# A hybrid decoder layer: low parts of the output weights moved behind the attention's divisions, first input blocks loaded in halves

## The chip, the cores and the metric

One NeuronCore of a Trainium2 chip runs the whole layer. The time is the device time of one execution in microseconds (us). TensorE multiplies matrices into PSUM; VectorE, ScalarE and GpSimd do elementwise work on SBUF (GpSimd not on PSUM); SyncE (SP) and ScalarE issue the transfers used here. Each engine takes its instructions in the order in which the program lists them.

## The reference

x is 512 x 1024, in float32. The layer is

```
h = rmsnorm(x, norm_g);  p = h @ w_in            # 1024 x 3380, split by columns
y_gla  = rmsnorm(gated linear attention(p)) * silu(gate)      # 4 heads, 384 channels
y_dsa  = sparse softmax attention(p) * silu(gate)             # 6 heads of 64
         # per query the 128 keys with the highest indexer score; softmax(q k / 8 + T5 bias)
y_pool = pooling mixer(p) * silu(gate)                        # 256 channels
out = rmsnorm(x + [y_gla, y_dsa, y_pool] @ w_out, final_norm_g)
```

## The kernel before, in words

Every product with a weight is made of three: an operand is split into a high part (a copy in the matmul's own format, `hi_of`, on ScalarE) and a low part (what the copy lost, `lo_of`, mostly on VectorE), and high x high, low x high and high x low are added in PSUM. 512 tokens are 4 tiles of 128, 1024 model columns are 8 blocks of 128.

**Opening** (`open_run`, L927). It multiplies the transposed, unnormalised x by the first 512 columns of w_in, block by block over the 8 blocks of the model dimension. Block k is a tile of x (128 x 512) and one of w_in (128 x 512). Block 0 of x comes with the 8 columns of norm_g behind it in one transfer (x0, L940); w0 and w1 are issued by ScalarE, all else by SP. Before its products TensorE runs four matmuls on ones (L991, 512, 512, 256 and 128 columns; each is two passes). `split(k)` (L949) makes the high part of w (whk, ScalarE), the high part of x times norm_g (hTh: VectorE for block 0, ScalarE for the others), the low part of x (hTl, VectorE) and the low part of w (wlk, VectorE). `square(k)` adds up x squared for the norm, on ScalarE and GpSimd. `products(k)` (L967) runs 3 x 4 matmuls of 512 columns.

**Projections** (`project`, L1017). The rest of w_in comes in chunks of some 256 columns, in the order qd, n1 to n4, dg, pg, c2, c1, pu, c0; each is loaded in two halves. Between the groups of matmuls a dictionary of hooks, `after` (L622), lists by hand what every engine is given next: ("pu", 0, "mid") is what comes in the middle of the first group of chunk pu, ("pu", 0) what comes after it. The order of these lists is the order of each engine's queue.

**Attention steps.** `att(...)` calls them by a letter, the query tile and the pair of heads ("n02" is n for tile 0, pair 2). l (L683): mask and bias into L, GpSimd, two instructions for tiles 2 and 3. q (L699): scores on TensorE, maximum on VectorE, exponentials with their sums on ScalarE. n (L715): reciprocal of the sums on VectorE (L719), then two multiplications on GpSimd (L721). t (L724): transposes of L on TensorE, copied out by ScalarE and VectorE. v (L734): values on TensorE (ov), times the gate on VectorE (yt), high part on ScalarE. y (L747): low part on VectorE.

**Output weights.** w_out comes in four chunks wo0 to wo3. `out_high(n, h)` (L901) makes the high parts of one half of chunk n on ScalarE, two instructions into tiles oh; `out_low(n, h)` (L909) the low parts ol, two instructions on VectorE. The tiles of the output weights take over memory that earlier tiles have left, so their first writes also wait for the last readers of those.

**Finish** (`finish`, L815). `out_part` adds the output products of one token tile: kinds G (linear attention), P (pooled, which wants yPh and yPl), D (softmax attention). Between them stand the attention steps of pairs 1 and 0 and the remaining parts of the weights, again in an order written out by hand. `pool_low` (L599) makes yPl, two VectorE instructions.

Of the kernel before, what the change touches and what calls it, by code (L numbers as in the profile page):

```python
# [69 lines left out]
def hybrid_layer(  # L70
# [16 lines left out]
    def S(tag, shape, dt=F32, bufs=1, name=None):  # L87
        return sb.tile(shape, dt, tag=tag, name=name or tag, bufs=bufs)
# [529 lines left out]
    def phase(n):  # L618
# [47 lines left out]
        ("c1", 1): [lambda: nc.gpsimd.memset(up[:, :, 0:16], 0.0), *att("l02", "l12"), partial(topk, 1, 3)],  # L666
        ("c1", 1, "end"): [*halves("c01"), partial(topk, 16, 2, 3)],
        ("pu", 0, "mid"): [*att("q02"), lambda: out_high(0, 0)],
        ("pu", 0): [lambda: out_low(0, 0), *att("n02", "q12")],
        ("pu", 1, "mid"): [*att("t02", "n12", "l22"), lambda: out_high(1, 0)],  # L670
        ("pu", 1): [*att("v02", "t12", "l32", "q22"), lambda: out_low(1, 0), lambda: pool_branch(0)],
        ("c0", 0, "mid"): att("n22", "y02", "v12", "q32"),
        ("c0", 0): att("t22", "n32", "l01"),
        ("c0", 0, "end"): [lambda: load_next(), *att("y12")],
        ("c0", 1, "mid"): [*att("v22", "t32", "l11"), lambda: pool_branch(1)],
# [139 lines left out]
    def finish():  # L815

        def do(*names):
            for f in att(*names):
                f()
# [12 lines left out]
        nc.sync.dma_start(lt["fg"], final_g.rearrange("(o d) -> o d", o=1).broadcast_to([P, D]))  # L832
        out_open(0), out_open(1)
        out_part(2, 0, T, "G", first=True)
        do("v01", "t11", "n21", "q00", "l10")
        pool_low()
        out_part(0, 0, T, "P")
        do("y01", "v11", "t21", "n00", "q31", "l20")
        out_low(2, 0)
        out_high(3, 0)  # L840
        out_part(1, 0, T, "P")
        do("y11", "v21", "t00", "n31", "q10", "l30")
        out_low(3, 0)
        out_high(2, 1)
        out_part(2, 0, T, "P")
        do("v00", "y21", "t31", "y00", "n10", "q20")
        out_low(2, 1)
        out_high(3, 1)
        out_part(0, 0, T, "D", last=True)
# [77 lines left out]
    def open_run():  # L927
# [3 lines left out]
        pns = [PS("ov", [P, T], 1, name="pf0"), PS("sc", [P, T], 2, name="pf1"), PS("sc", [P, T], 2, name="pf2"),  # L931
               PS("pj", [P, T], 3, name="pf3")]
        ht = lambda parts, k: parts[k // 4][:, k % 4, :]
        x0 = S("x0", [P, T + KT])
        g_of = lambda k: x0[:, T + k:T + k + 1]

        def load_x(k):
            if k == 0:
                xs[0] = x0[:, 0:T]
                nc.sync.dma_start(x0, block(x_t, 0, T + KT))  # L940
                return
            xs[k] = S("xk", [P, T], bufs=5, name=f"xk{k}")
            nc.sync.dma_start(xs[k], block(x_t, k * P * T + P * KT, T))

        def load_w(k, eng=nc.sync):
            ws[k] = S("wk", [P, T], bufs=5, name=f"wk{k}")
            eng.dma_start(ws[k], block(w_in, k * P * T, T))

        def split(k):  # L949
            wh[k] = S("whk", [P, T], F32R, bufs=3, name=f"whk{k}")  # L950
            wl[k] = S("wlk", [P, T], F32R, bufs=3, name=f"wlk{k}")
            hi_of(wh[k], ws[k])
            if k:
                nc.scalar.activation(ht(hTh, k), xs[k], AF.Copy, scale=g_of(k))
            else:
                nc.vector.tensor_scalar(ht(hTh, k), xs[k], g_of(k), None, op0=ALU.mult)
            nc.vector.scalar_tensor_tensor(ht(hTl, k), xs[k], g_of(k), ht(hTh, k).bitcast(F32),
                                           op0=ALU.mult, op1=ALU.subtract)
            lo_of(wl[k], ws[k], wh[k])
# [7 lines left out]
        def products(k, parts=range(3)):  # L967
            for part in parts:
                a, w = ht(hTl if part == 1 else hTh, k), (wl if part == 2 else wh)[k]
                for t in range(NT):  # L970
                    mm(pns[t], a[:, t * P:(t + 1) * P], w, start=(k + part == 0),  # L971
                                    stop=(k == KT - 1 and part == 2))

        def rms():

# [12 lines left out]
        nc.sync.dma_start(tab, table)  # L988
        load_next()
        load_next()  # L990
        for n in (4, 4, 2, 1):  # L991
            mm(warm[:, 0:n * P], ones, ones4[:, 0:n, :], start=True, stop=True)
        split(0)
        square(0)
# [76 lines left out]
def _x_blocks(x_t, norm_g):  # L1071

    import numpy as np

    first = np.concatenate([x_t[0:P], norm_g.reshape(KT, P).T], axis=1)
    return np.concatenate([first.reshape(-1), x_t[P:].reshape(-1)])


def _blocks(w, cols):
# [6 lines left out]
def _layout(i):  # L1086
    import numpy as np

    i = {n: np.asarray(a) for n, a in i.items()}
    w_in, w_out = i["w_in"][0], i["w_out"][0]  # L1090
    return {
        "in_x": i["x"],
        "in_x_t": _x_blocks(i["x"][0].T, i["norm_g"][0]),
        "in_w_in": np.concatenate([w_in[:, FIRST].reshape(-1)] + [_blocks(w_in, cols) for _, cols in CHUNKS]),
        "in_w_out": np.concatenate([_blocks(w_out, list(range(256 * j, 256 * j + 256))) for j in range(4)]),
        "in_rel_bias": _bias_layout(i["rel_bias"]),
        "in_table": _small_layout(i["gla_gate_w2"], i["gla_gate_b"], i["gla_norm_g"], i["pool_w"], i["pool_scale"]),
        "in_final_g": i["final_norm_g"],
    }
# [24 lines left out]
```

## Time and profile before

| | |
|---|---|
| median of 3 runs | 263.54 us (262.72 to 264.03) |
| the profiled execution | 262.61 us, span 260.7 us |
| mean granted clock of TensorE | 0.987 |
| TensorE busy | 245.6 us, 94% of the span |
| VectorE busy | 198.2 us, 76% |
| ScalarE, GpSimd busy | 119.0 us, 46%; 105.5 us, 40% |

In the rows, PE is TensorE, PEld its weight loads, DVE VectorE, ACT ScalarE, POOL GpSimd and SPq the issue of a transfer by SP. A row of a timeline gives start and duration in us, engine, line, operation, what is written from what, sizes, how many instructions are merged in it (x) and, in brackets, how long the engine was idle before it and whose result ended that. A matmul's row includes its way through the array, so rows of one engine overlap. PEclk is the share of TensorE's full clock that was granted.

### The profile page before, as it was taken

Reading aid. Unit: us, or ns where it says so; the run is one execution under the profiler, and the core shown is the slowest. Engines: PE = TensorE matmul, PEld = TensorE weight load, DVE = VectorE, ACT = ScalarE, POOL = GpSimd, SP = SyncE. Lnnn points to the kernel's source line nnn. Section 1 sums busy time; section 2 is a strip of 40 time slices with the busy share of each in tenths; the row PEclk is TensorE's granted clock in tenths of the full one; section 3 lists DMA queues with packets and bytes.
Section 4 is the critical chain, followed back from the end, with each engine's and each line's share of the span. In section 5 each row is a group of like instructions: output and inputs, shape, how many; then the busy total and the mean of one; then the engine's idle time right before and its main releaser. Section 6 shows DMA issues by size and latency. Waiting matters only on the chain.

```text
span 260.7 us, 4198 instructions
## 1 busy us (share of the span) xinstructions
PE 245.6 (94%) x1498; PEld 204.9 (79%) x1498; DVE 198.2 (76%) x442; ACT 119.0 (46%) x251; POOL 105.5 (40%) x109
## 2 busy tenths in 40 slices
PE   8999999999999999999999996699998989999990
PEld 4778889999999998778888884477875757778890
DVE  3999488999999999996999862288789797345322
ACT  5964186884836724062223452324168457222111
POOL 1644356253067730438534070534618783000011
PEclk9999999999999999999999999799999999999997
DMA  7994413226203150222325887500669000035012
GB/s 246 394 411 152 129 45 97 72 67 235 77 1 93 70 165 3 80 80 83 88 73 115 194 211 194 177 1 19 195 148 365 3 1 0 3 106 207 36 56 80
DMA packets 11780, 31.09 MB, mean 119 GB/s; under 512 B 1600, under 2 KB 1600, under 8 KB 11760
## 3 DMA queue, kind: packets, MB, share of 16 engines
q1 hardware_dynamic: 11328, 30.05, 36.2%
q10 hardware_dynamic: 432, 0.79, 0.8%
q8 instruction: 12, 0.20, 0.4%
q14 instruction: 8, 0.07, 0.1%
HBM read 23.91 MB, written 2.10 MB: 100 GB/s over the span
## 4 chain that ended last, share of the span: by engine, by line
PE 54%; DVE 30%; DMA 6%; issue 5%; POOL 2%; ACT 1%; POOLq 0%; ACTq 0%; DVEq 0%
PE op L772 14%; DVE scs L459 8%; DVE m L458 6%; PE pf L971 5%; PE pt_c L210 4%; PE pt_c L208 4%; PE pt_c L209 4%; DMA wr_wo<-in_w_out 3%; PE tpp L730 3%; PE ov L741 3%; PE ps L708 2%; DVE scs L444 2%; DMA wk<-in_w_in 2%; DVE wl_n L99 2%; PE pt_pg L210 1%
## 5 line engine op out<-in xcount | busy, mean ns | idle before, releaser
L721 POOL TENSOR_SCALAR L<-L,ast 128x128 f32<-128x128 f32 (+3 forms) x24 | 15.0, 639 | 32.5 <-DVE ast L719 32.5
L458 DVE MAX8 m<-scs 128x8 f32<-128x256 f32 (+2 forms) x48 | 26.5, 552 | 0.1
L459 DVE MATCH_REPLACE8 scs<-m,scs 128x256 f32<-128x256 f32 (+2 forms) x48 | 26.0, 543 | 0.0
L196 PE MATMUL pn_n<-wh_n,hTh 128*128 128x270 f32 (+1 forms) x128 | 21.6, 291 | 0.0
L196 PE MATMUL pn_n<-wl_n,hTh 128*128 128x270 f32 (+1 forms) x128 | 21.2, 287 | 0.0
L196 PE MATMUL pn_n<-wh_n,hTl 128*128 128x270 f32 (+1 forms) x128 | 21.0, 286 | 0.0
L208 PE MATMUL pt_c<-hTh,wh_c 128*128 128x512 f32 x48 | 19.2, 400 | 0.0
L210 PE MATMUL pt_c<-hTh,wl_c 128*128 128x512 f32 x48 | 19.0, 395 | 0.0
L209 PE MATMUL pt_c<-hTl,wh_c 128*128 128x512 f32 x48 | 18.9, 395 | 0.0
L196 PEld LDWEIGHTS pn_n<-wh_n,hTh 128*128 128x128 f32 x128 | 18.2, 189 | 0.7 <-issue 0.4
L712 ACT ACTIVATE L<-L,ast 128x128 f32<-128x128 f32 (+3 forms) x24 | 13.3, 554 | 11.8 <-DVE ast L710 10.7
L196 PEld LDWEIGHTS pn_n<-wl_n,hTh 128*128 128x128 f32 x128 | 18.0, 189 | 0.0
L196 PEld LDWEIGHTS pn_n<-wh_n,hTl 128*128 128x128 f32 x128 | 18.0, 189 | 0.0
L99 DVE TENSOR_TENSOR ol<-wr_wo,oh 128x512 fp32r<-128x512 f32 x16 | 12.8, 837 | 6.6 <-ACT oh L96 3.9
L99 POOL TENSOR_TENSOR wl_c<-wr_c,wh_c 128x1024 fp32r<-128x1024 f32 x5 | 12.0, 2401 | 12.9 <-PE pt_c L210 8.7
L730 PE MATMUL tpp<-ident,L 128*128 128x128 f32 x60 | 9.7, 288 | 6.3 <-POOL L L721 6.2
L965 POOL TENSOR_TENSOR acc<-acc,sqk 128x512 f32<-128x512 f32 x7 | 10.6, 1513 | 10.9 <-ACT sqk L963 10.8
L730 PEld LDWEIGHTS tpp<-ident,L 128*128 128x128 f32 x60 | 6.6, 142 | 9.4 <-POOL L L721 7.9
L96 ACT ACTIVATE yDh<-yt 128x128 fp32r<-128x128 f32 x12 | 3.7, 308 | 21.9 <-DVE yt L744 21.9
L558 POOL TENSOR_TENSOR gss<-gss,hneg 128x4 f32<-128x4 f32 x4 | 5.0, 1238 | 21.3 <-DVE gss L557 18.5
L778 ACT ACTIVATE sqo<-xr 128x512 f32<-128x512 f32 (+1 forms) x8 | 4.8, 605 | 17.9 <-DVE xr L777 12.9
L689 POOL TENSOR_TENSOR L<-scs,TB 128x512 f32<-128x512 f32 x9 | 12.9, 1438 | 0.0
(241 smaller groups left out, 710.7 us busy)
## 6 DMA issues: line engine op xcount, KB each, us to landing
wr_wo<-in_w_out SPq DMA_DIRECT2D x8, 512.0 KB, 4.2
wr_c<-in_w_in SPq DMA_DIRECT2D x6, 512.0 KB, 3.6
wr_n<-in_w_in SPq DMA_DIRECT2D x4, 540.0 KB, 7.8
wr_n<-in_w_in SPq DMA_DIRECT2D x4, 536.0 KB, 3.5
xr<-in_x SPq DMA_DIRECT2D x4, 512.0 KB, 6.0
xk<-in_x_t SPq DMA_DIRECT2D x7, 256.0 KB, 5.4
wk<-in_w_in SPq DMA_DIRECT2D x6, 256.0 KB, 5.2
KK<-qkh SPq DMA_DIRECT2D x12, 128.0 KB, 2.5
```

Source lines behind the costliest of these rows:

```text
L99: return (eng or nc.vector).tensor_tensor(dst, src, hi.bitcast(F32), op=ALU.subtract)
L196: mm(ps[:, 0:n], a[:, k, ts_], w[:, k, :], start=(h + part + k == 0), stop=(h == 1 and part == 2 and k == 3))
L208: mm(ps[:, t0:T], c.hi[h][:, k, cs], hTh[h][:, k, t0:T], start=(h + k == 0), stop=False)
L209: mm(ps[:, t0:T], c.hi[h][:, k, cs], hTl[h][:, k, t0:T], start=False, stop=False)
L210: mm(ps[:, t0:T], c.lo[h][:, k, cs], hTh[h][:, k, t0:T], start=False, stop=(h == 1 and k == 3))
L458: nc.vector.max(out=m8, in_=msk[i])
L459: nc.vector.match_replace(out=msk[i], in_to_replace=m8, in_values=msk[i], imm_value=TAKEN)
L712: nc.scalar.activation(L[:, b, 0:n], L[:, b, 0:n], AF.Exp, bias=st[:, b:b + 1], scale=-1.0, accum_out=st[:, 2 + b:3 + b])
L721: nc.gpsimd.tensor_scalar(L[:, b, 0:n], L[:, b, 0:n], st[:, 4 + b:5 + b], 1.0, op0=ALU.mult, op1=ALU.mult)
L730: nc.tensor.transpose(tp[:, kb, :], L[:, b, kb * P:(kb + 1) * P], ident)
L772: mm(outs[t][a][:, 0:e - a], lhs, rhs, start=(first and yi == 0 and rhs is wh and lhs is yh), stop=(last and yi == len(ys) - 1 and lhs is yl))
L971: mm(pns[t], a[:, t * P:(t + 1) * P], w, start=(k + part == 0), stop=(k == KT - 1 and part == 2))
```

## The change

In the hooks, out_low(0,0) moves from the start of ("pu", 0) to the end of ("pu", 1, "mid"), ahead of out_high(1,0); out_low(1,0) moves from ("pu", 1) to the end of ("c0", 0, "mid"). In the finish, pool_low moves ahead of v01, t11, n21, q00 and l10; l20 and l30 move to the end of the next lists. In the opening the first block of x (with norm_g now in front) and the first block of w_in come in two transfers of 256 columns each, their high parts are made in two halves and the first products in eight matmuls of 256 columns; the warm-up keeps its first two matmuls of four.

```diff
-        ("pu", 0): [lambda: out_low(0, 0), *att("n02", "q12")],
-        ("pu", 1, "mid"): [*att("t02", "n12", "l22"), lambda: out_high(1, 0)],
-        ("pu", 1): [*att("v02", "t12", "l32", "q22"), lambda: out_low(1, 0), lambda: pool_branch(0)],
-        ("c0", 0, "mid"): att("n22", "y02", "v12", "q32"),
+        ("pu", 0): att("n02", "q12"),
+        ("pu", 1, "mid"): [*att("t02", "n12", "l22"), lambda: out_low(0, 0), lambda: out_high(1, 0)],
+        ("pu", 1): [*att("v02", "t12", "l32", "q22"), lambda: pool_branch(0)],
+        ("c0", 0, "mid"): [*att("n22", "y02", "v12", "q32"), lambda: out_low(1, 0)],
...
+        pool_low()
         do("v01", "t11", "n21", "q00", "l10")
-        pool_low()
         out_part(0, 0, T, "P")
-        do("y01", "v11", "t21", "n00", "q31", "l20")
+        do("y01", "v11", "t21", "n00", "q31")
         out_low(2, 0)
         out_high(3, 0)
         out_part(1, 0, T, "P")
-        do("y11", "v21", "t00", "n31", "q10", "l30")
+        do("y11", "v21", "t00", "n31", "q10", "l20")
         out_low(3, 0)
         out_high(2, 1)
         out_part(2, 0, T, "P")
-        do("v00", "y21", "t31", "y00", "n10", "q20")
+        do("v00", "y21", "t31", "y00", "n10", "q20", "l30")
...
+                nc.sync.dma_start(x0[:, 0:KT + H], block(x_t, 0, KT + H))
+                nc.sync.dma_start(x0[:, KT + H:KT + T], block(x_t, P * (KT + H), H))
...
+            if k == 0:
+                for a in (0, H):
+                    eng.dma_start(ws[0][:, a:a + H], block(w_in, a * P, H))
...
+                for a in (0, H):
+                    hi_of(wh[0][:, a:a + H], ws[0][:, a:a + H])
+                    nc.vector.tensor_scalar(ht(hTh, 0)[:, a:a + H], xs[0][:, a:a + H], g_of(0), None, op0=ALU.mult)
...
+                if k + part == 0:
+                    for t, c in ((0, 0), (1, 0), (0, H), (1, H), (2, 0), (3, 0), (2, H), (3, H)):
+                        mm(pns[t][:, c:c + H], a[:, t * P:(t + 1) * P], w[:, c:c + H], start=(c == 0), stop=False,
+                           skip_group_check=True)
...
-        for n in (4, 4, 2, 1):
+        for n in (4, 4):
```

H is 256. The layout of x and w_in in memory follows the halves.

## Rows read from the trace of the kernel before

**Rows 1.** The page: span

```profile
span 260.7 us, 4198 instructions
```

**Rows 2.** Timeline, 150 to 172 us: the pu stage

```profile
157.15 0.69 DVE L388 TENSOR_TENSOR up<-pt_pu,rsb 128x512 f32<-128x512 f32 x1 [1.09 <-PE pt_pu L210]
...
160.17 1.15 ACT L96 ACTIVATE oh<-wr_wo 128x512 fp32r<-128x512 f32 x2 [3.40 <-PE pt_pu L209]
...
164.19 0.69 DVE L99 TENSOR_TENSOR ol<-wr_wo,oh 128x512 fp32r<-128x512 f32 x1 [2.67 <-DMA KL<-qkl]
...
165.13 0.72 POOL L721 TENSOR_SCALAR L<-L,ast 128x128 f32<-128x128 f32 x2 [8.34 <-DVE ast L719]
...
165.55 0.82 PE L730 MATMUL tpp<-ident,L 128*128 128x128 f32 x2 [5.19 <-POOL L L721]
...
166.87 0.93 POOL L721 TENSOR_SCALAR L<-L,ast 128x256 f32<-128x256 f32 x2 [1.02 <-DVE ast L719]
```

**Rows 3.** Windows: us; busy of PE, PEld, DVE, ACT, POOL; PEclk; DMA share, GB/s

```profile
165.50:168.70 3.20, 3.15 (x8) 2.44 (x9) 0.49 (x4) 2.11 (x7) 2.18 (x4) 0.50 0.31 127
```

**Rows 4.** Timeline, 166 to 185 us: the end of pu and the c0 stage

```profile
166.47 1.15 ACT L96 ACTIVATE oh<-wr_wo 128x512 fp32r<-128x512 f32 x2
...
170.32 0.69 DVE L388 TENSOR_TENSOR up<-pt_pu,rsb 128x512 f32<-128x512 f32 x1 [3.54 <-PE pt_pu L210]
...
171.46 0.35 ACT L732 COPY pt<-tpp 128x256 f32<-128x256 f32 x1
...
172.69 1.29 DVE L99 TENSOR_TENSOR ol<-wr_wo,oh 128x512 fp32r<-128x512 f32 x2
...
174.66 0.66 PE L741 MATMUL ov<-pt,dv 128*64 128x128 f32 x8
...
177.72 1.14 POOL L721 TENSOR_SCALAR L<-L,ast 128x384 f32<-128x384 f32 x2 [5.86 <-DVE ast L719]
...
179.07 0.81 PE L730 MATMUL tpp<-ident,L 128*128 128x128 f32 x6
...
180.65 1.91 POOL L721 TENSOR_SCALAR L<-L,ast 128x512 f32<-128x512 f32 x2 [1.79 <-DVE ast L719]
...
183.43 1.09 PE L730 MATMUL tpp<-ident,L 128*128 128x128 f32 x8
```

**Rows 5.** Timeline, 194 to 222 us: the finish

```profile
199.71 0.28 DVE L744 TENSOR_TENSOR yt<-ov,dg 128x128 f32<-128x128 f32 x1
...
200.68 2.21 POOL L721 TENSOR_SCALAR L<-L,ast 128x384 f32<-128x384 f32 x2
...
200.72 1.59 DVE L99 TENSOR_TENSOR yPl<-pg,yPh 128x512 fp32r<-128x512 f32 x2
...
201.46 0.50 PE L772 MATMUL op<-oh,yPl 128*128 128x512 f32 x1 [0.93 <-DVE yPl L99]
...
206.11 2.47 DVE L99 TENSOR_TENSOR ol<-wr_wo,oh 128x512 fp32r<-128x512 f32 x2
...
209.35 2.31 POOL L721 TENSOR_SCALAR L<-L,ast 128x512 f32<-128x512 f32 x2 [1.32 <-DVE ast L719]
...
211.72 0.66 PE L730 MATMUL tpp<-ident,L 128*128 128x128 f32 x4 [0.96 <-POOL L L721]
```

**Rows 6.** Timeline, 0 to 28 us: the opening

```profile
1.04 4.54 PE L992 MATMUL warm<-ones 128*128 128x512 f32 x8 [1.04 <-DVE lead L108]
...
1.16 0.42 SPq L943 DMA_DIRECT2D xk<-in_x_t  x1
...
5.33 1.19 PE L971 MATMUL pf<-whk,hTh 128*128 128x512 f32 x4
...
5.71 0.63 ACT L96 ACTIVATE whk<-wk 128x512 fp32r<-128x512 f32 x1 [0.16 <-DMA wk<-in_w_in]
...
16.31 1.20 PE L971 MATMUL pf<-wlk,hTh 128*128 128x512 f32 x4 [0.33 <-DVE wlk L99]
```

**Rows 7.** Windows, as in rows 3: the warm-up's first part

```profile
1.00:4.60 3.60, 3.56 (x4) 1.51 (x5) 0.38 (x1) 1.70 (x3) 0.29 (x1) 1.00 0.78 251
```

More of the change, by code (lines that the diff above doesn't have):

```diff
@@ L933, in open_run @@
         ht = lambda parts, k: parts[k // 4][:, k % 4, :]
-        x0 = S("x0", [P, T + KT])
-        g_of = lambda k: x0[:, T + k:T + k + 1]
+        x0 = S("x0", [P, KT + T])
+        g_of = lambda k: x0[:, k:k + 1]
+        H = T // 2
         def load_x(k):
             if k == 0:
-                xs[0] = x0[:, 0:T]
-                nc.sync.dma_start(x0, block(x_t, 0, T + KT))
+                xs[0] = x0[:, KT:KT + T]
+                nc.sync.dma_start(x0[:, 0:KT + H], block(x_t, 0, KT + H))
+                nc.sync.dma_start(x0[:, KT + H:KT + T], block(x_t, P * (KT + H), H))
                 return
@@ L946, in load_w @@
             ws[k] = S("wk", [P, T], bufs=5, name=f"wk{k}")
+            if k == 0:
+                for a in (0, H):
+                    eng.dma_start(ws[0][:, a:a + H], block(w_in, a * P, H))
+                return
             eng.dma_start(ws[k], block(w_in, k * P * T, T))
@@ L951, in split @@
             wl[k] = S("wlk", [P, T], F32R, bufs=3, name=f"wlk{k}")
-            hi_of(wh[k], ws[k])
             if k:
+                hi_of(wh[k], ws[k])
                 nc.scalar.activation(ht(hTh, k), xs[k], AF.Copy, scale=g_of(k))
             else:
-                nc.vector.tensor_scalar(ht(hTh, k), xs[k], g_of(k), None, op0=ALU.mult)
+                for a in (0, H):
+                    hi_of(wh[0][:, a:a + H], ws[0][:, a:a + H])
+                    nc.vector.tensor_scalar(ht(hTh, 0)[:, a:a + H], xs[0][:, a:a + H], g_of(0), None, op0=ALU.mult)
             nc.vector.scalar_tensor_tensor(ht(hTl, k), xs[k], g_of(k), ht(hTh, k).bitcast(F32),
@@ L969, in products @@
                 a, w = ht(hTl if part == 1 else hTh, k), (wl if part == 2 else wh)[k]
+                if k + part == 0:
+                    for t, c in ((0, 0), (1, 0), (0, H), (1, H), (2, 0), (3, 0), (2, H), (3, H)):
+                        mm(pns[t][:, c:c + H], a[:, t * P:(t + 1) * P], w[:, c:c + H], start=(c == 0), stop=False,
+                           skip_group_check=True)
+                    continue
                 for t in range(NT):
-                    mm(pns[t], a[:, t * P:(t + 1) * P], w, start=(k + part == 0),
-                                    stop=(k == KT - 1 and part == 2))
+                    mm(pns[t], a[:, t * P:(t + 1) * P], w, start=False, stop=(k == KT - 1 and part == 2),
+                       skip_group_check=True)
         def rms():
@@ L1073, in _x_blocks, with _first @@
     import numpy as np
-    first = np.concatenate([x_t[0:P], norm_g.reshape(KT, P).T], axis=1)
-    return np.concatenate([first.reshape(-1), x_t[P:].reshape(-1)])
+    first = np.concatenate([norm_g.reshape(KT, P).T, x_t[0:P, 0:T // 2]], axis=1)
+    return np.concatenate([first.reshape(-1), x_t[0:P, T // 2:].reshape(-1), x_t[P:].reshape(-1)])
+def _first(w):
+    import numpy as np
+    return np.concatenate([w[0:P, 0:T // 2].reshape(-1), w[0:P, T // 2:].reshape(-1), w[P:].reshape(-1)])
 def _blocks(w, cols):
@@ L1093, in _layout @@
         "in_x_t": _x_blocks(i["x"][0].T, i["norm_g"][0]),
-        "in_w_in": np.concatenate([w_in[:, FIRST].reshape(-1)] + [_blocks(w_in, cols) for _, cols in CHUNKS]),
+        "in_w_in": np.concatenate([_first(w_in[:, FIRST])] + [_blocks(w_in, cols) for _, cols in CHUNKS]),
         "in_w_out": np.concatenate([_blocks(w_out, list(range(256 * j, 256 * j + 256))) for j in range(4)]),
```

## The prediction, made before the change was run

> **What bounds the kernel now.** I read the page first: a span of 260.7 us [rows 1]. Its table of engines gives TensorE the largest share, but that says nothing yet of where time can be saved, so the views by place come next. The list of waits, taken for TensorE alone, has one large entry; the timeline around it shows who made it wait. In the pu stage TensorE ends a group of projections at about 160.4 and then stands for 5.19 us, until the transposes of t02 start at 165.55 [rows 2]. They need n02, the division by the softmax sum: a reciprocal on VectorE and two multiplications on GpSimd. GpSimd starts these at 165.13, after 8.34 us of idling for VectorE [rows 2]. VectorE was not busy. It finished the evacuation of the first pu half at 157.84 and then stood in front of out_low(0,0), which the program puts ahead of n02: its first half waits for ScalarE's high parts (160.17 and on, themselves held 3.40 us until TensorE has read the old contents of the buffer), its second until 164.19 for the KL transfers, and the reciprocal comes behind it [rows 2]. The reader should see a queue in the wrong order: the low parts are wanted only at the output products at about 188, the division at once.
>
> The windows show the second cost: after that idle stretch, from 165.5 to 168.7, the granted clock is 0.50 [rows 3].
>
> The stage after it, c0, has no TensorE wait on another engine, but two close hand-overs from VectorE through GpSimd, t22 and t32 [rows 4]. In the finish two waits remain: 0.93 us for yPl, the low parts of the pooled branch, and 0.96 us for t31 [rows 5]. The opening is bound by VectorE: the first products start at 5.33, but the low parts of block 3 come only at 16.3, and TensorE waits 0.33 us for them [rows 6].
>
> **The change, part by part.** All sums are against the profiled execution, 262.61 us with its span of 260.7; the median of the runs shown is 263.54, 0.93 more.
>
> *Two out_low moves in the pu stage.* out_low(0,0) (two VectorE instructions, no transfer) goes behind n02, q12, t02, n12 and l22. n02's exponentials are done long before, so the reciprocal follows the evacuation at 157.84; GpSimd needs 0.72 us [rows 2] and is done by about 158.9, before TensorE arrives at 160.4. The 5.19 us go. With them goes the slow stretch: the same columns take half as long at full clock, so 3.2 us at 0.50 [rows 3] cost about 1.5. Together 6.7 us at the start of the c0 stage.
>
> What is late next? out_low(0,0) still cannot end before 164.19 + 0.69 = 164.88, since the KL transfers do not move. Behind it on VectorE now stand the second pu evacuation, v02's product, t12's copy, q22 and the pool scans, then n22. Before, VectorE went without a gap from that evacuation at 170.32 to the start of n22 on GpSimd at 177.72: 7.40 us, of which out_low(1,0), which the change moves away, was about 1.2 [rows 4]. So n22 starts on GpSimd at 164.9 + 6.2 = 171.1 and ends 1.14 later at 172.2. TensorE comes to t22 at 179.07 - 6.7 = 172.4. No wait, by 0.2 us. out_low(1,0) now stands behind q32, that is ahead of the next evacuation and of n32: from n22 to n32 on GpSimd it was 180.65 - 177.72 = 2.93, now 4.2, so n32 starts at 175.3 and ends 1.91 later at 177.2; TensorE comes to t32 at 183.43 - 6.7 = 176.7 plus its own later losses [rows 4]. That is a wait of up to 0.5. A third place is ScalarE: out_high(1,0) keeps its place, its load had landed by 166.47, and it takes 1.15 [rows 4]; if the load came just then, v12's copy on ScalarE, behind it and one other short operation of at most 0.35 like itself, is ready at 168.3, where TensorE comes to v12 at 174.66 - 6.7 = 168.0. A wait of 0.3 (0 to 0.5). For t22 and t32 I charge 0.4 together, between none and the case where VectorE works at its contended prices (below). q12's exponentials stand on ScalarE behind out_high(0,0), which ends at 161.3; from VectorE's release at 165.1 to the end of n12 at 167.80 it took 2.7 with the exponentials in it [rows 2], so n12 is now done by about 163.9, and TensorE, after t02, twelve projections and v02, wants it at about 164.
>
> Stage: 6.7 - 0.3 - 0.4 = 6.0 us.
>
> *The finish.* pool_low (two VectorE instructions, 1.59 us together) moves ahead of v01, t11, n21 and q00, so it starts where v01's product stood, at 199.71, 1 us earlier; TensorE's wait of 0.93 and a shorter one behind it go [rows 5]. But v01's product, t11's copy and the reciprocal of n21 stand behind it, about 1.4 later. n21 on GpSimd started at 200.68 and took 2.21, beside pool_low on VectorE [rows 5]. It now starts at about 202.1 and, with no such neighbour, takes nearer to the 1.14 that the same form took for n22 [rows 4]: done at 203.3 instead of 202.9. TensorE, 1.1 early, waits there for t21. Of 1.1 us I keep 0.3.
>
> l20 and l30 (two GpSimd instructions each) move behind n31 and n10. l20 ran beside out_low(2,0), which took 2.47 where out_low(1,0) took 1.29 [rows 4, 5]; alone it ends some 1.2 earlier. The reciprocal of n31 follows it, so n31 starts at 209.35 - 1.2 - 0.3 = 207.9 and ends by 210.2 even at its old 2.31; TensorE arrives for t31 at about 210.4 and its wait of 0.96 goes [rows 5]. l20 then ends at about 212.5, l30 at 216: VectorE takes q20 and q30 there, 1.3 earlier than it did. Finish: 0.3 + 1.0 = 1.3 us.
>
> *The opening.* x0 and w0 come in halves, one more issue on SP (0.42 us [rows 6]) and one on ScalarE's queue. The first products need half of each and the warm-up, whose four 512-column passes end at 4.61 [rows 7]; so they start about 0.7 earlier than 5.33. This gains nothing later. VectorE's chain from block 1 on sets 16.3, and it starts when w1 has landed (ScalarE's whk at 5.71 waited for that transfer [rows 6]). The bytes ahead of w1 are the same, so its landing stays. TensorE waits longer at the same low parts. The next loads leave SP 0.4 later but stand in line for the same transfer engines anyway. No row has half-size blocks: the bounds are a gain of 0.7, if the whole chain moves up, and a loss of 0.8, two more issues of 0.42 in front of the chain. I take 0, since the row nearest to it, whk, waits for a landing and not for an issue.
>
> TensorE's clock: the four warm-up passes took 3.56 us [rows 7]; the trace has TensorE busy from 1.04 on without a break [rows 6]. With half of each block in hand before 4.61 the products follow the shorter warm-up at once, so I assume the same rise. The Trainium skill, "TensorE: Matmul & The Clock Gate", Part 1, says that throttled is the default and activity releases it, and its section "Why this matters for your kernels" advises to warm up first and to keep TensorE busy without breaks; a shorter one speaks against the change. By that rule another slow stretch, like the one of 3.2 us here, would cost 1.5 on TensorE, of which its longer waits in the opening hide about one.
>
> *Sum:* 6.0 + 1.3 + 0 = 7.3 us. 262.6 - 7.3 = 255.3 for an execution like the profiled one; from the median, 263.5 - 7.3 = **256.2**.
>
> **Rivals.** A: VectorE becomes the bound of the c0 stage. For it: the hand-overs t22 and t32 have 0.2 and -0.5 us to spare in my sum, and VectorE's operations stretch beside GpSimd's (2.47 against 1.29 for the same pair [rows 4, 5]). If the four low parts and the scans stretch so, VectorE is 3 us later and TensorE waits it out: 263.5 - 4.3 = 259.2. Against it: the pair in the c0 stage took 1.29 with GpSimd at rest. Chance 0.16, of which 0.03 for so much more that under 0.5% is left.
>
> B: all waits go and the opening moves up too: 6.7 + 1.1 + 1.0 + 0.7 = 9.5, 254.0. Against it: whk's wait for w1. Chance 0.09.
>
> C, slower: the clock. Products start on half blocks while the clock has not risen, TensorE then stands for VectorE, and the clock stays at 0.50. A stretch costs half its length [rows 3]; it must eat the 7.3 and the 0.7 + 0.33, about 1 us, by which TensorE would else wait longer for VectorE [rows 6], so it decides from some 17 us on, to beyond 21 us. At 20 us: 10 - 1 - 7.3 = 1.7 slower, 265.2. Against it: the wait of TensorE for VectorE at 16.31 is 0.33 [rows 6], and with 0.7 more it stays short of the 5.19 that went before the slow stretch [rows 2, 3]. Chance 0.05.
>
> **Numbers.** My forecast has 0.70, with an own range of 254.8 to 257.6. Rivals 0.16, 0.09 and 0.05. The range 253.8 to 259.4 reaches to B and to A and leaves out A's worst, C and half of B, about 0.13. A measurement of this kernel can tell about 0.5% (1.3 us) from no change: faster 0.92, same 0.03, slower 0.05.
>
> **What would show it.** Right: the 5.19 us wait at tpp is gone, the granted clock stays at full speed from the opening to the last stage, VectorE's second low part still ends near 164.9 but with the reciprocal ahead of it, t31 no longer waits and t21 does, low parts of block 3 still come near 16.3. Wrong: a wait of over 1 us at t22 or t32 (A), first products that pull the end of the opening forward (B), or a clock of 0.50 after 8 us (C).

## The result, and the profile after the change

| | before | changed kernel |
|---|---|---|
| median of 4 runs each | 263.13 us (262.27 to 264.03) | 259.62 us (259.53 to 259.78) |
| ratio, with its 95% interval | | 0.9867 (0.983 to 0.9903) |
| the profiled execution | 262.61 us, span 260.7 | 259.53 us, span 257.7 |
| mean granted clock of TensorE | 0.987 | 0.996 |

The change gains 3.5 us, where 7.3 were forecast; 259.62 lies 0.2 above the range. The page, span and granted clock in 40 slices: the slow stretch of [rows 3] is gone.

```profile
span 257.7 us, 4207 instructions
...
PEclk9999999999999999999999999999999999999998
```

**The pu and c0 stages** went nearly as forecast. Timeline, 159 to 167 us and 168 to 182 us, and the window that answers to the 5.19 us of [rows 2] (columns as in [rows 3]):

```profile
159.61 0.69 DVE L388 TENSOR_TENSOR up<-pt_pu,rsb 128x512 f32<-128x512 f32 x1 [1.07 <-PE pt_pu L210]
...
160.22 0.15 DVE L719 RECIPROCAL ast<-ast 128x2 f32<-128x2 f32 x1
...
160.47 0.73 POOL L721 TENSOR_SCALAR L<-L,ast 128x128 f32<-128x128 f32 x2 [1.20 <-DVE ast L719]
...
162.68 0.38 PE L730 MATMUL tpp<-ident,L 128*128 128x128 f32 x2
...
164.81 0.17 DVE L719 RECIPROCAL ast<-ast 128x2 f32<-128x2 f32 x1 [1.42 <-ACT L L712]
164.89 1.27 DVE L99 TENSOR_TENSOR ol<-wr_wo,oh 128x512 fp32r<-128x512 f32 x2
...
165.07 1.82 POOL L721 TENSOR_SCALAR L<-L,ast 128x256 f32<-128x256 f32 x2 [3.87 <-DVE ast L719]
...
165.77 0.44 PE L741 MATMUL ov<-pt,dv 128*64 128x128 f32 x4
...
166.48 0.78 PE L730 MATMUL tpp<-ident,L 128*128 128x128 f32 x3 [0.27 <-POOL L L721]
```

```profile
170.78 0.66 PE L741 MATMUL ov<-pt,dv 128*64 128x128 f32 x8
...
175.20 0.90 PE L730 MATMUL tpp<-ident,L 128*128 128x128 f32 x6
...
179.62 1.32 PE L730 MATMUL tpp<-ident,L 128*128 128x128 f32 x8
```

```profile
160.00:165.00 5.00, 5.00 (x25) 4.02 (x24) 1.53 (x9) 2.28 (x7) 0.73 (x2) 1.00 0.92 217
```

The reciprocal now follows the evacuation of 159.61 at once, GpSimd is done at 161.2, and TensorE, busy for all 5 us of the window at clock 1.00, takes t02 at 162.68 without a wait. The reader should subtract the starts of one instruction in both traces, for that shows where time comes and goes. t02: 162.68 - 165.55 = -2.87 [rows 2]. v12: 170.78 - 174.66 = -3.88. t22: 175.20 - 179.07 = -3.87. t32: 179.62 - 183.43 = -3.81 [rows 4].

One hand-over between these starts became late, that of t12. Before, v02 and t12 started thus:

```profile
170.21 0.44 PE L741 MATMUL ov<-pt,dv 128*64 128x128 f32 x4
...
170.58 0.66 PE L730 MATMUL tpp<-ident,L 128*128 128x128 f32 x4
```

v02 starts 4.44 earlier in the changed kernel, t12 only 4.10, after a wait of 0.27 for n12 with a second wait of 0.25 in the middle of t12, and from v12 on the gain is 3.9. The divisions of n12 now stand beside the low parts of out_low(0,0) and take 1.82, where they took 0.93 [rows 2].

**The opening** explains why t02 is only 2.87 earlier. Timeline, 0 to 9 us, of TensorE to 22 us, and two rows of TensorE between 30 and 40 us, the one of before and the one of the changed kernel:

```profile
1.16 0.42 SPq L942 DMA_DIRECT2D x<-in_x_t  x1
...
1.63 0.43 SPq L945 DMA_DIRECT2D xk<-in_x_t  x1
1.64 0.45 ACTq L953 DMA_DIRECT2D wk<-in_w_in  x1
...
4.04 2.49 PE L980 MATMUL pf<-whk,hTh 128*128 128x256 f32 x8
...
7.69 0.63 ACT L96 ACTIVATE whk<-wk 128x512 fp32r<-128x512 f32 x1 [2.51 <-DMA wk<-in_w_in]
```

```profile
18.28 1.19 PE L984 MATMUL pf<-wlk,hTh 128*128 128x512 f32 x4 [0.32 <-DVE wlk L99]
```

```profile
35.03 1.13 PE L925 MATMUL rb<-diag,ones 128*128 128x512 f32 x2
```

```profile
37.51 1.12 PE L925 MATMUL rb<-diag,ones 128*128 128x512 f32 x2 [0.46 <-DVE qil L99]
```

The first products start 1.3 earlier than before (4.04 and 5.33 [rows 6]), but ScalarE waits 2.51 us for w1 and begins its high part at 7.69 instead of 5.71, and the low parts of block 3 come at 18.28 instead of 16.31 [rows 6]: +1.97, handed on by VectorE's chain. A little later TensorE waits another 0.46 for VectorE, at 37.51, which it didn't before; from there on the delay is 2.5, and the evacuation in the pu stage still has it, 159.61 - 157.15 = 2.46 [rows 2]. So t02 gained 2.87 + 2.46 = 5.33 in the pu stage, v12 3.88 + 2.46 = 6.34, with the slow stretch, and t32 3.81 + 2.46 = 6.27.

**The end of c0 and the finish** give back 1 us. Three rows of before and then those of the changed kernel:

```profile
173.89 2.44 DVE L583 TENSOR_TENSOR_SCAN pm<-up 64x512 f32<-64x512 f32 x2
...
185.16 2.83 DVE L583 TENSOR_TENSOR_SCAN pm<-up 64x512 f32<-64x512 f32 x2
...
189.12 0.68 DVE L367 SCALAR_TENSOR_TENSOR qkr<-pt_c,rsb 128x512 f32<-128x512 f32 x1
```

```profile
181.58 3.52 DVE L583 TENSOR_TENSOR_SCAN pm<-up 64x512 f32<-64x512 f32 x2
...
186.47 0.68 DVE L367 SCALAR_TENSOR_TENSOR qkr<-pt_c,rsb 128x512 f32<-128x512 f32 x1
...
191.86 0.14 PEld L730 LDWEIGHTS tpp<-ident,L 128*128 128x128 f32 x1 [0.97 <-POOL L L721]
```

```profile
194.75 2.41 DVE L99 TENSOR_TENSOR ol<-wr_wo,oh 128x512 fp32r<-128x512 f32 x2
...
197.08 2.13 DVE L99 TENSOR_TENSOR yPl<-pg,yPh 128x512 fp32r<-128x512 f32 x2
...
198.66 0.51 PE L772 MATMUL op<-oh,yPl 128*128 128x512 f32 x1 [0.78 <-DVE yPl L99]
```

```profile
207.37 1.09 PE L730 MATMUL tpp<-ident,L 128*128 128x128 f32 x8
...
217.15 0.50 PE L772 MATMUL op<-ol,yPh 128*128 128x512 f32 x1 [0.68 <-DVE ol L99]
```

VectorE's second pair of scans of the pooled branch now runs wholly beside GpSimd and takes 3.52 instead of 2.83, when it ran partly beside it (the first pair of before, at 173.89, took 2.44 with GpSimd at rest). So the evacuation of the c0 group comes at 186.47, only 2.65 earlier, where the scans had begun 3.58 earlier. VectorE sets the pace from there: TensorE's weight load waits 0.97 for n01, and then 0.78 for yPl, which was 0.93 [rows 5]; at that product the gain is 201.46 - 198.66 = 2.80. t31 runs in one piece, its 0.96 us [rows 5] are gone, but a new wait of 0.68 for the low parts of out_low(3,1) stands at 217.15. The span ends 3.0 shorter.

### The profile page after: what moved, and what is told of

It is laid out like the page before. It is cut to its first block, busy times and chain, and to the rows that moved or that the text cites. A ratio compares the mean times of both kernels' runs of the same rounds, so it can differ in the third digit from the quotient of the medians.

```text
span 257.7 us, 4207 instructions
## 1 busy us (share of the span) xinstructions
PE 246.1 (95%) x1498; PEld 203.9 (79%) x1498; DVE 199.9 (78%) x443; ACT 119.2 (46%) x252; POOL 108.4 (42%) x109
## 4 chain that ended last, share of the span: by engine, by line
PE 39%; DVE 35%; issue 6%; POOL 3%; ACT 1%; POOLq 0%; DVEq 0%; ACTq 0%
PE op L772 10%; DVE scs L459 8%; DVE m L458 6%; PE pt_c L210 4%; PE pt_c L209 4%; PE pt_c L208 4%; DVE ol L99 3%; PE tpp L730 2%; PE ov L741 2%; DVE wl_n L99 2%; DVE L L710 2%; PE pt_pg L210 1%; PE pt_pg L208 1%; PE pt_pg L209 1%; DVE scs L444 1%
## 5 line engine op out<-in xcount | busy, mean ns | idle before, releaser
L721 POOL TENSOR_SCALAR L<-L,ast 128x128 f32<-128x128 f32 (+3 forms) x24 | 14.6, 619 | 24.9 <-DVE ast L719 22.4
L689 POOL TENSOR_TENSOR L<-scs,TB 128x512 f32<-128x512 f32 x9 | 14.7, 1642 | 0.0
L96 ACT ACTIVATE qkh<-qkr 128x512 fp32r<-128x512 f32 x6 | 3.8, 633 | 20.7 <-DVE qkr L367 11.0
L99 POOL TENSOR_TENSOR wl_n<-wr_n,wh_n 128x1080 fp32r<-128x1080 f32 (+1 forms) x4 | 10.1, 2531 | 5.7 <-ACT wh_n L96 4.9
L777 DVE TENSOR_TENSOR xr<-op,xr 128x512 f32<-128x512 f32 (+1 forms) x8 | 5.2, 654 | 9.0 <-PE op L772 9.0
```

The source lines that it names most:

```text
L99: return (eng or nc.vector).tensor_tensor(dst, src, hi.bitcast(F32), op=ALU.subtract)
L689: nc.gpsimd.tensor_tensor(L[:, :, near], msk[i][:, near].unsqueeze(1).to_broadcast([P, 2, 256]), TB[:, 2 * g:2 * g + 2, :], op=ALU.subtract)
L721: nc.gpsimd.tensor_scalar(L[:, b, 0:n], L[:, b, 0:n], st[:, 4 + b:5 + b], 1.0, op0=ALU.mult, op1=ALU.mult)
```

## The experiments

"The orders alone" below is the changed kernel with the opening of before. Medians of one group of runs share the runs of before; between groups the ratios are to be compared.

### Parts of the change

**The orders alone.** Diff against the changed kernel: its opening taken back (x0 and w0, their high parts and products whole, and the long warm-up).

```diff
-                nc.sync.dma_start(x0[:, 0:KT + H], block(x_t, 0, KT + H))
-                nc.sync.dma_start(x0[:, KT + H:KT + T], block(x_t, P * (KT + H), H))
+                nc.sync.dma_start(x0, block(x_t, 0, T + KT))
...
-        for n in (4, 4):
+        for n in (4, 4, 2, 1):
```

> The changed hooks and finish with the opening of before. Theory: the opening's delay (TensorE's rb 2.5 us later than before) is carried to the end and adds to the rest, so without it the time is 259.6 - 2.5 = 257.1 us (256.6 to 257.7), 0.977 of before, with block 3's low parts back at about 16.3. Rival: the delay is absorbed later, since the stages behind the opening have waits of their own; then the time stays near 259.6.

Measured: 257.54 us (256.88 to 257.75) beside 262.96 of before, ratio 0.9794 (0.9763 to 0.9825). The first theory holds: without the opening's part, the gain is 5.4 us, 1.9 more than the whole change has (0.9867 - 0.9794 = 0.0073, of 263).

**The opening alone.** Diff against before: the changed kernel's opening, hooks and finish as before.

```diff
-                nc.sync.dma_start(x0, block(x_t, 0, T + KT))
+                nc.sync.dma_start(x0[:, 0:KT + H], block(x_t, 0, KT + H))
+                nc.sync.dma_start(x0[:, KT + H:KT + T], block(x_t, P * (KT + H), H))
...
-        for n in (4, 4, 2, 1):
+        for n in (4, 4):
```

> Before with the halves and the shorter warm-up, old hooks and finish. Theory: the delay of 2.5 us appears whole at the end, 263.1 + 2.5 = 265.6 us (265.0 to 266.2). Rival: the waits of the pu stage (5.2 us, for the KL transfers' landing and VectorE) absorb it, 263.1 to 264.

Measured: 261.44 us (260.83 to 262.55) beside 262.96, ratio 0.9946 (0.9924 to 0.9968). My theory falls: alone, the opening costs nothing, it even gains, and the time lies below the rival's 263.1 to 264 too. Timeline, the high part of w1, VectorE around out_low(0,0), and t02:

```profile
7.18 0.63 ACT L96 ACTIVATE whk<-wk 128x512 fp32r<-128x512 f32 x1 [2.08 <-DMA wk<-in_w_in]
```

```profile
162.82 1.29 DVE L99 TENSOR_TENSOR ol<-wr_wo,oh 128x512 fp32r<-128x512 f32 x2 [2.98 <-ACT oh L96]
164.03 0.16 DVE L719 RECIPROCAL ast<-ast 128x2 f32<-128x2 f32 x1
```

```profile
164.79 0.68 PE L730 MATMUL tpp<-ident,L 128*128 128x128 f32 x2 [2.43 <-POOL L L721]
```

w1 comes 1.5 later than in before, but TensorE's wait at t02 is 2.43 instead of 5.19, and t02 starts 0.76 earlier. TensorE arrives there 2.00 later than in before (164.79 - 2.43 = 162.36 against 165.55 - 5.19 = 160.36 [rows 2]), so the wait took in the whole delay; with it gone the delay reaches the end. The 0.76 have another source: here the low parts run in one piece and the reciprocal follows at 164.03, while in before the second half stood until 164.19 for the KL transfers [rows 2]. Why it does not stand here is not shown, so the 0.9946 is not the opening's own worth.

**The warm-up.** Diffs: the first against the changed kernel, the second against the orders alone.

```diff
-        for n in (4, 4):
+        for n in (4, 4, 2, 1):
```

```diff
-        for n in (4, 4, 2, 1):
+        for n in (4, 4):
```

> The changed kernel with the warm-up of before (512, 512, 256 and 128 columns). Theory, the transfers: w1 still lands near 7.66 and block 3's low parts come near 18.3, so the time is 259.6 (259.2 to 260.0), although the clock rises nearer to 4.9 than to 6.76. Rival, the clock: with full speed from 4.9 on the opening is back where it was, 257.1.

> The orders alone, with whole first blocks, but with the shorter warm-up (two matmuls of 512 columns). Theory, the transfers: w1 lands near 5.7 and the time is that of the orders alone, 257.1 (256.6 to 257.7). Rival, the clock: the loss comes from the shorter warm-up, 259.6.

Measured, in the group of the first two: 258.18 us (257.84 to 258.36), ratio 0.9821 (0.9791 to 0.9851), with the halves and the long warm-up; 257.33 us (257.18 to 257.97), ratio 0.9795 (0.9764 to 0.9825), with whole blocks and the short one. The short warm-up by itself costs nothing. The first is in between: w1's high part starts at 6.91 there. The clock did not rise earlier for the longer warm-up: its trace has the full clock on record from 6.67, the changed kernel's from 6.76, where I expected nearer to 4.9. That the long warm-up gives back some 1.2 of the halves' loss (0.9821 and 0.9867) was expected by neither theory, so the changed kernel was run again below.

### What in the halves costs

**Small packets in one transfer; two transfers of whole rows.** Diffs against the orders alone, shown for w0 (x0 likewise; `halves` reads two runs of half rows):

```diff
-            eng.dma_start(ws[k], block(w_in, k * P * T, T))
+            if k == 0:
+                eng.dma_start(ws[0].rearrange("p (a c) -> p a c", a=2), halves(w_in, T // 2))
```

```diff
+                for a in (0, 64):
+                    eng.dma_start(ws[0][a:a + 64, :], block(w_in, a * T, T)[0:64])
```

> The orders alone, and x0 and w0 each in one transfer whose packets are half rows (256 instead of 128 per transfer); everything else is whole as before. Same issues, same bytes, twice the packets. Theory A, the number of packets: what is behind them in the queue comes as late as with the halves, w1 lands at 7 or later and the opening loses 1.2 to 2.5 us, 258.7 to 260.0. Rival B, the extra issues and the limited number of transfers in flight: nothing of that is here, so w1 lands near 5.6 and the time is 257.5 (257.0 to 258.0).

> The orders alone, and x0 and w0 each in two transfers of 64 partitions, with whole rows. The issues of the change, x1 and w1 0.45 us later on their queues, but the packets of before. Theory A, the number of packets: w1 lands near 5.6 and the time is 257.5 (257.0 to 258.0). Rival B, the extra issues: w1 lands at 7 or later, 258.7 to 260.0.

Measured: 257.19 us (257.11 to 257.29), ratio 0.9819 (0.9795 to 0.9843), and 259.85 us (259.4 to 262.17), ratio 0.9927 (0.9903 to 0.995). Timelines, the high part of w1 in the one, those of w0 and w1 in the other:

```profile
5.75 0.63 ACT L96 ACTIVATE whk<-wk 128x512 fp32r<-128x512 f32 x1 [0.31 <-DMA wk<-in_w_in]
```

```profile
6.00 0.63 ACT L96 ACTIVATE whk<-wk 128x512 fp32r<-128x512 f32 x1 [2.27 <-DMA wk<-in_w_in]
...
7.84 0.63 ACT L96 ACTIVATE whk<-wk 128x512 fp32r<-128x512 f32 x1 [0.69 <-DMA wk<-in_w_in]
```

My first idea, the number of packets, falls: 256 half packets in one transfer move nothing, and two transfers with the packets of before cost 2.7 us. In the second more differs than that: w0 itself is handed on late, at 6.00 (4.19 in the orders alone), and x1 was issued later than in the changed kernel, at 1.97. The Trainium skill, "DMA: Bandwidth & Descriptors", Rules for kernel authors, advises against two transfers for the two halves of the partitions, since they share the same engines; the run agrees, 259.85 beside the 257.19 of one transfer, and here the two do not only gain nothing but cost.

**Extra transfers, held-back transfers, a later issue.** Diffs against the orders alone: a transfer of 256 bytes ahead of x1 on SP's queue and one ahead of w1 on ScalarE's; both on SP's queue ahead of w3; w1 issued by SP behind x1.

```diff
+        tiny(0, nc.sync), tiny(1, nc.scalar)
         for k in range(1, KT):
```

```diff
         for k in range(1, KT):
+            if k == 3:
+                tiny(0, nc.sync), tiny(1, nc.sync)
```

```diff
-            load_w(k, nc.scalar if k == 1 else nc.sync)
-            load_x(k)
+            if k == 1:
+                load_x(k)
+                load_w(k)
+                continue
+            load_w(k)
+            load_x(k)
```

> The orders alone with whole first blocks, and one tiny extra transfer (256 bytes) ahead of x1 on SP's queue and one ahead of w1 on ScalarE's. No more bytes and only two more packets. Theory, extra transfers ahead: they cost by their number, not by what they carry; x1 and w1 are issued 0.45 us later and find six transfers where there were four, so w1 lands at 6.5 or later and the time is 258.5 to 260.0. Rival, the load of the halves themselves (packets and waits of the engines for them): nothing of that is here, 257.4.

> The same two tiny transfers, but on SP's queue behind x2, ahead of w3. x1, w1, w2 and x2 are issued when they were; w3 and x3 become the ninth and tenth transfer and are issued only when the first ones have landed, as in the changed kernel. Theory, extra transfers ahead of x1 and w1: w1 lands near 5.6 and the time is that of the orders alone, 257.4. Rival, the eight transfers in flight: with w3 and x3 held back too few bytes are in line and the loads come late, 258.5 to 260.0.

> The orders alone with whole first blocks; w1 is issued by SP behind x1 instead of by ScalarE, so 0.4 us later (near 1.62 instead of 1.22), w2 and all behind it 0.45 later too. No extra transfer. Theory, the number of transfers: an issue that is 0.4 later lands at most 0.4 later, 257.4 to 257.9. Rival, the issue time alone (whatever is issued at 1.6 misses the turn of the transfer engines): w1 lands at 6.5 or later, 258.5 to 260.0.

Measured, beside 262.11 of before: 257.34 us (256.22 to 257.9), ratio 0.9802 (0.9755 to 0.9848); 257.02 us (256.19 to 257.09), 0.9787 (0.9745 to 0.9829); 257.51 us (257.31 to 257.74), 0.9816 (0.9769 to 0.9864). None has the loss (the first theory of the tiny transfers falls), and w1's high part starts at 5.66, 5.58 and 5.73. So it is not the later issue of x1 or of w1, not the mere number of transfers when the added ones are this small, and not w3 and x3 being issued late (at 4.21 and 4.62 in the second, where the changed kernel has w3 at 3.56).

**The halves as transfers only; x0 alone in halves; the changed kernel again.** Diffs against the orders alone: the loads of x0 and w0 as in the changed kernel, all else whole and the long warm-up; of these the load of x0 only. The changed kernel is as it was.

```diff
-                nc.sync.dma_start(x0, block(x_t, 0, T + KT))
+                nc.sync.dma_start(x0[:, 0:KT + H], block(x_t, 0, KT + H))
+                nc.sync.dma_start(x0[:, KT + H:KT + T], block(x_t, P * (KT + H), H))
...
+            if k == 0:
+                for a in (0, H):
+                    eng.dma_start(ws[0][:, a:a + H], block(w_in, a * P, H))
+                return
```

```diff
-                nc.sync.dma_start(x0, block(x_t, 0, T + KT))
+                nc.sync.dma_start(x0[:, 0:KT + H], block(x_t, 0, KT + H))
+                nc.sync.dma_start(x0[:, KT + H:KT + T], block(x_t, P * (KT + H), H))
```

> The orders alone with x0 and w0 in two transfers of 256 columns each, but whole high parts, whole products and the long warm-up of before. Theory, half-sized transfers: w1 lands at 6.9 or later and the time is that of the changed kernel on this chip within 0.5, some 258.2 to 259.6. Rival, the halved products or the warm-up: 257.4.

> As the run before, but only x0 in two transfers; w0 is whole. Theory, half-sized transfers: each queue's next transfer is ready no sooner behind a half than behind a whole one; w0's whole packets still fill the transfer engines, so the loss is half or less of that with both, 257.4 to 258.3. Rival, the issue order on SP (x1 and all behind it 0.45 later is enough): the whole loss, as with both.

> The changed kernel once more, beside the next three on one chip. Theory, the landings: the warm-up costs nothing, and what the changed kernel loses to the one with the long warm-up (1.4 us) comes from landings that differ with the chip; then it takes 258.2 to 259.0 here, and w1 lands where it lands with the halves as transfers only. Rival, the warm-up: 259.6 here too, 1 us or more above the halves as transfers only.

Measured, beside 262.92 of before: 258.85 us (258.7 to 259.05), ratio 0.9835 (0.9797 to 0.9873); 256.98 us (256.32 to 257.24), 0.9767 (0.9722 to 0.9811); 259.29 us (258.8 to 260.05), 0.9854 (0.9812 to 0.9895). Windows of the changed kernel, of the halves as transfers only, of x0 alone in halves and of the orders alone (the last column is what the transfers moved, in GB/s):

```profile
3.50:4.50 1.00, 1.00 (x3) 0.29 (x1) 0.71 (x3) 0.67 (x2) 0.00 (x0) 1.00 0.87 218
4.50:5.50 1.00, 1.00 (x6) 0.89 (x5) 1.00 (x2) 0.68 (x2) 0.00 (x0) 1.00 0.71 246
```

```profile
3.50:4.50 1.00, 1.00 (x2) 0.34 (x1) 0.31 (x1) 0.10 (x1) 0.00 (x0) 1.00 0.93 226
4.50:5.50 1.00, 1.00 (x4) 0.71 (x3) 0.96 (x3) 1.00 (x2) 0.00 (x0) 1.00 1.05 277
```

```profile
3.50:4.50 1.00, 1.00 (x3) 0.41 (x2) 0.00 (x0) 0.48 (x1) 0.00 (x0) 1.00 1.11 381
4.50:5.50 1.00, 0.86 (x6) 0.64 (x5) 0.71 (x2) 0.90 (x3) 0.00 (x0) 1.00 1.09 299
```

```profile
3.50:4.50 1.00, 1.00 (x2) 0.34 (x1) 0.49 (x1) 0.31 (x1) 0.00 (x0) 1.00 1.04 387
4.50:5.50 1.00, 1.00 (x4) 0.71 (x3) 0.96 (x2) 0.84 (x2) 0.00 (x0) 1.00 1.02 389
```

And the high part of w1 with the halves as transfers only, with x0 alone in halves, and in the orders alone:

```profile
7.68 0.63 ACT L96 ACTIVATE whk<-wk 128x512 fp32r<-128x512 f32 x1 [2.13 <-DMA wk<-in_w_in]
```

```profile
5.28 0.61 ACT L96 ACTIVATE whk<-wk 128x512 fp32r<-128x512 f32 x1
```

```profile
5.58 0.63 ACT L96 ACTIVATE whk<-wk 128x512 fp32r<-128x512 f32 x1 [0.23 <-DMA wk<-in_w_in]
```

This settles which part of the change loses. With the first block of both queues in half-sized transfers, the transfers move 218 and 246 GB/s from 3.5 to 5.5 (226 and 277 with nothing but the transfers changed), where whole ones move 387 and 389, although x1, w1, w2 and x2 are all issued by 3.1; w1 is handed on at 7.68 instead of 5.58. With x0 alone in halves the transfers move 381 up to 4.5 and 299 behind it, and nothing is lost; w0 alone in halves was not run. What the transfers moved is not the whole of it: in the changed kernel with the long warm-up they moved 370 and 363 GB/s in these two windows, and w1's high part still started at 6.91; in its trace 14 of w1's 16 parts have landed by 5.84, the last at 6.88. So single parts of a block land late, and the block is whole only with the last of them; the GB/s alone do not tell the loss. What goes with it in every trace is w1: its high part starts at 6.9 or later wherever the first blocks of both queues came in two transfers, and by 5.8 wherever they did not. The changed kernel's 259.29 lie above its theory's 258.2 to 259.0, and its w1 at 8.24 is later than the 7.68 with the halves as transfers only; they lie less than 1 us above that version, so its rival does not hold either. Of the 259.29, 258.85 are there without the halved products and the short warm-up; the ranges of the two overlap, so what the warm-up adds beside the halves, 0.4 here and some 1.2 between the two groups, stays open: in the profiled executions it went with w1 (7.69 and 8.24 with the short warm-up, 6.91 and 7.68 with the long one, but 7.18 with the short one in the opening alone).

### The finish

**pool_low back; l20 and l30 back; the hooks only.** Diffs against the orders alone: pool_low behind v01, t11, n21, q00, l10 as before; l20 and l30 at their old places; both.

```diff
-        pool_low()
         do("v01", "t11", "n21", "q00", "l10")
+        pool_low()
```

```diff
-        do("y01", "v11", "t21", "n00", "q31")
+        do("y01", "v11", "t21", "n00", "q31", "l20")
...
-        do("y11", "v21", "t00", "n31", "q10", "l20")
+        do("y11", "v21", "t00", "n31", "q10", "l30")
...
-        do("v00", "y21", "t31", "y00", "n10", "q20", "l30")
+        do("v00", "y21", "t31", "y00", "n10", "q20")
```

> The orders alone, but pool_low back behind v01, t11, n21, q00 and l10. Theory: moving it gained next to nothing, since VectorE reaches it only after out_low(1,1) and it then runs beside GpSimd (2.13 us for the pair instead of 1.59): 257.5 (257.1 to 258.1). Rival, my forecast's step: 0.3 us slower, 257.8, not to be told from it by the time; the trace decides, by whether TensorE's wait for yPl (0.77 in the orders alone) is over 1 us.

> The orders alone, but l20 and l30 back at their old places. Theory: the move is a wash, it takes t31's wait away (0.96) and sets l30 beside out_low(2,1), which takes 2.46 instead of 1.38, so that TensorE waits 0.68 for out_low(3,1): 257.5 (257.1 to 258.1), with t31's wait back and the wait for ol under 0.2. Rival, my forecast's step: the move is worth 1.0, 258.5.

> Before with the two moves of low parts in the pu and c0 stages only; finish and opening as before. Theory: the finish's moves are a wash, so the time is that of the orders alone, 257.4 (257.0 to 257.9), with TensorE's waits for yPl (0.9) and t31 (1.0) as before. Rival, my forecast's sum: 6.0 of the gain is here and 1.3 in the finish, 258.7.

Measured: 256.9 us (256.8 to 257.0), ratio 0.9808 (0.9784 to 0.9832); 257.59 us (257.37 to 257.73), 0.9834 (0.9809 to 0.9858); 257.6 us (257.44 to 257.66), 0.9786 (0.9749 to 0.9823). The first two stand in the group of the small packets, which had both moves and 257.19: by that, moving pool_low costs some 0.3 and moving l20 and l30 gains some 0.4. These two sizes are not shown: that run has the small packets besides, and against the orders alone, in another group (0.9794), pool_low back is no gain at all (0.9808). The trace was to decide, by TensorE's wait for yPl with pool_low back:

```profile
196.21 0.50 PE L772 MATMUL op<-oh,yPl 128*128 128x512 f32 x1 [0.92 <-DVE yPl L99]
```

It is not over 1 us (0.77 in the orders alone), so the theory holds, though 256.9 lies 0.2 below its range: the move gained next to nothing. The hooks alone have the whole gain of the orders (0.9786 and 0.9794). With l20 and l30 back, t31's wait returns and that for ol goes; waits of TensorE there:

```profile
PE tpp L730 <- POOL L L721: 1.0, 1, 1.0
PE op L772 <- DVE yPl L99: 0.8, 1, 0.8
```

### A version to beat both

**The order of the pooled products.** Diff against the orders alone: in `out_part`, of the chunks 6 and 7 (the pooled branch), the product with yPl comes last in the first half of the columns, the one with the low weights last in the second.

```diff
-            for lhs, rhs in ((yh, wh), (yh, wl), (yl, wh)):
+            todo = [(yh, wh), (yh, wl), (yl, wh)]
+            if c >= 6:
+                back += [todo.pop(2 if a == 0 else 1)]
+            if c == 7:
+                todo += back
+            for lhs, rhs in todo:
```

> A version to beat both: the orders alone, and in the products of the pooled branch those with the late operand (yPl in the first half of the columns, the low parts of the weights in the second) come last. TensorE's waits for yPl (0.77 and a shorter one) and for ol (0.68) should shrink by two products each, 0.46: 256.6 (256.2 to 257.2) where the orders alone have 257.4. If the time is then taken by the next step of VectorE, 257.4.

Measured, in the group of the tiny transfers: 256.41 us (256.37 to 256.64), ratio 0.9773 (0.9734 to 0.9813). The waits that it was to shrink did shrink: TensorE's wait for yPl falls from 0.77 to 0.30, and its list of waits has none for ol any more. In the time the step from the orders alone (0.9794) is too small to tell, for the two intervals overlap. The wait for yPl:

```profile
196.14 1.10 PE L778 MATMUL op<-oh,yPl 128*128 128x512 f32 x2 [0.30 <-DVE yPl L99]
```

**With x0 alone in halves too.** The diff is that of the run before and that of x0 alone in halves, together.

> The orders alone, the pooled branch's late operands last, and x0 alone in two transfers. Theory, both gains are real and add up: 0.9773 of before for the product order, less another 0.4 us, so 0.975 to 0.977, 256.0 (255.6 to 256.5). Rival, x0's two transfers moved nothing and the 0.4 is scatter of the landings: 256.5, 0.977 to 0.979.

Measured: 256.36 us (255.5 to 257.6) beside 262.25, ratio 0.9781 (0.974 to 0.9821). The rival holds: x0's two transfers add nothing that can be told. The order of the products with whole first blocks is the version to keep, 5.7 us faster than before and about 2.5 faster than the changed kernel (0.9773 and 0.9867). Most of that are the hooks' moves; that the order of the products adds to them shows in the waits and not yet in the time.

## Why the prediction was right in the orders and wrong in the rest

1. *The two out_low moves: right.* 6.0 us were forecast for the pu and c0 stages; in the changed kernel the start of t32 shows 3.81 + 2.46 = 6.27. The 5.19 us wait is gone, the clock stays up and the reciprocal stands ahead. One sign did not come: the second low part was to end near 164.9, held by the KL transfers; the pair only starts at 164.89, behind n12's reciprocal, and ends at 166.16. The hooks alone are worth 5.3 us at the end (257.6 and 262.92).
2. *t22, t32 and v12: the losses came elsewhere, and the 6.0 is in part luck.* Up to v02 the gain is 4.44 + 2.46 = 6.9, where 6.7 were forecast. 0.3 were charged for v12 and 0.4 for t22 and t32, whose starts lose less than 0.1 to each other. What was lost is some 0.5 at t12, for which the forecast charged nothing: it had n12 done by 163.9 just ahead of TensorE, and n12's divisions only start at 165.07, beside the low parts.
3. *Rival A: a small part of it came, at another place.* VectorE's scans at the end of c0 stretch from 2.83 to 3.52 beside GpSimd, and from the c0 evacuation on VectorE sets the pace: 1.0 of the stage's gain is gone at yPl (6.27 at t32, 2.80 + 2.46 = 5.26 there). No wait over 1 us came at t22 or t32, the places that the rival named.
4. *The finish: the term was mis-sized,* 1.3 forecast, none that can be told measured (0.9786 for the hooks alone, 0.9794 for the orders). pool_low starts ahead of v01's product, as I said, but there its pair runs beside GpSimd and takes 2.13 instead of 1.59, and v01's product and t11's copy come behind it. The 0.93 for yPl was to go, and 0.78 of it stayed: I moved VectorE forward as far as TensorE, and it was not. t21 did not become the wait I named. Of l20 and l30 the wait for t31 went as said, but I charged nothing for the place they moved to: TensorE now waits 0.68 for out_low(3,1), and with both back at their old places that wait is gone.
5. *The opening: the step that failed.* "The bytes ahead of w1 are the same, so its landing stays", taken as 0 with a loss of at most 0.8. The bytes were the same; the landing moved by 2. The first products did start 1.3 earlier, and gained nothing, as I said. I took a row that waits for a landing as proof that only bytes decide it. Block 3, to stay near 16.3, came at 18.28, and the delay was 2.5 by the pu stage. The runs put the loss into the half-sized transfers on both queues, 1.3 us by themselves (258.85, and 257.6 for the hooks alone in the same group) and 1.7 to 1.9 in the changed kernel (259.29 in that group; 0.9867 against 0.9794 between groups). Why parts of x1 and w1 land so late is not shown.
6. *The clock: it stayed up, as assumed; what the short warm-up costs is open.* The Trainium skill, "TensorE: Matmul & The Clock Gate", section "Why this matters for your kernels", speaks for the longer warm-up. The rows agree as far as the products go: with whole blocks and the short one the first four products took 1.64 us instead of 1.19, and the trace has the full clock on record only from 5.98, 1.0 behind their start. But that lies under the hidden part of the opening, and the time stayed (0.9795 and 0.9794). So by itself it costs nothing that can be told; beside the halves, 0.4 to 1.2 us stay open, as said above.

Put together, against the 7.3: 5.3 from the hooks, 0 from the finish, about -1.9 from the opening, 3.4; measured 3.5. In the trace it is 6.3 at t32, 1.0 lost by yPl and 2.5 from the opening: 2.8 there.

## What to carry to other kernels

Order each engine's queue by who is waiting for the result, and look for the stage where a busy engine is held by an idle one that stands before work nobody needs yet. When the first loads are cut up to start sooner, look at when the *second* block lands. Here halves at the head of both queues cost, and halves of x0 alone did not; the other way round was not run. And test the parts of a change together as well as alone: a delay that one stage's wait swallows appears at the end as soon as that wait is removed.

## What the runs showed of the hardware

- Two transfers instead of one at the head of each of two queues, with the same bytes: from 3.5 to 5.5 us they and those behind them moved 218 and 246 GB/s (halves of the columns) or 215 and 238 (halves of the rows, the same packets) instead of 387 and 389. These figures are not the loss itself: with the long warm-up the halves had 370 and 363, and w1's high part still came at 6.91. In the changed kernel's trace the 16 parts of x1 land between 4.62 and 7.47, in before's between 4.54 and 5.50.
- Packets of 1 KB instead of 2 KB within one transfer cost nothing that can be seen (257.19, w1's high part at 5.75).
- VectorE's work stretches beside GpSimd's, by how much depends on what runs there: a pair of low parts took 1.27 us beside its divisions (L721), one of the same size 2.41 beside its two-operand instructions (L689), and the scans 2.44 with GpSimd at rest, 2.83 partly and 3.52 wholly beside it. The divisions pay in turn: 1.82 beside the low parts and 0.93 without. An engine off the path set the finish this way.
